# First MLP product of a diffusion step: units of 512 features, context tile as the stationary operand

## The chip, the cores and the metric

One core of a Trainium2 chip runs the whole step in one launch. The metric is the device time in microseconds (us) of one execution; lower is better. The engines are TensorE (PE in the profile; PEld is its loading of the stationary operand), VectorE (DVE), ScalarE (ACT), GpSimd (POOL) and SyncE (SP), from whose queue the DMA transfers of this kernel are issued. A matmul multiplies a stationary operand (here 128 columns, loaded into the array first) with a moving operand that streams past it column by column, and accumulates in a bank of PSUM (128 partitions x 512 float32).

## The reference

There is one layer. Its first part (norm, DeltaNet and gMLP heads, output projection) is not touched by the change. What follows it, for 128 context tokens `x` and 2048 latent tokens `y` of width 1024:

```python
h = rmsnorm(x, norm_ffn_l) * (1.0 + sc2) + sh2
x = x + ga2 * (jnp.square(jax.nn.relu(h @ w_ff1_l)) @ w_ff2_l)
...
y_prompt = rmsnorm(x, norm_final)
y_sample = rmsnorm(y, norm_final)
```

`w_ff1` is 1024 x 4096 and `w_ff2` 4096 x 1024. All is float32. The kernel reaches the accuracy with a split: each operand becomes a rounded part H and a remainder L, and a product is the three matmuls H·H, H·L and L·H (`mm3`, L214 to L220: lines 218, 219 and 220 are one matmul each, and all products of the kernel show up at these lines).

## The kernel before, in words

The tokens are 17 tiles of 128 rows: tile 0 is the context, tiles 1 to 16 are the latents. The stage in question is the first MLP product, from about 1298 us to 2023 us of the profiled span; the second MLP product follows, up to the end.

**Strassen-Winograd.** The 16 latent tiles are multiplied with seven products in place of eight. Tiles are paired (odd and even), features are split in two blocks (i = 0, 1) and the inner dimension of 1024 in two halves (kh = 0, 1). The moving operands, sums of token tiles for each of the seven products, come from DRAM as `hop` tiles (1 MB each, with parts H and L; `hop_next`, L899). Four pairs go side by side: 512 moving columns. There are two halves g of the work: g = 0 handles tiles 9 to 16, g = 1 tiles 1 to 8.

**Units.** `Unit` (L1470) takes 256 features: two blocks of 128, 16 units in each half. `loads` fetches four raw tiles of w_ff1 (one for each block and inner half; 128 x 512, 256 KB, rows of 128 floats). `weights(o)` forms the stationary operand of product o from them on DVE and splits it (`split4`, L1453: a cast on ACT, L1457, and a subtraction on DVE through the helper `add`, L1451). `product(o)` issues 4 inner tiles x 3 matmuls with the weights stationary and 512 moving columns. `step(o)` issues the product and evacuates it: copies and additions, the squared ReLU, stores to `z_d`, `s1_d` and `s2_d`, which the second MLP product reads as operands.

**The context tile.** It has no partner and is multiplied plainly, in the second half only, where the weights of a plain block are there anyway: `single` (L1566), for o in 1, 2, 0, 4, issues 12 matmuls with the weights stationary and the 128 context columns moving. Product 0 exists only for that. `single_out` applies the squared ReLU (ACT L1581, then a DVE multiplication) and stores to `z_d[0]`. `first_tile` loads the normed context tile from DRAM (`h2_0_d`) and splits it, ten steps ahead of the second half.

**Order.** `seq` (L1790) is the list of steps: for each unit its products in `ORDER` (1, 5, 6, 7, 3, 2, 4; in the second half 0 ahead of 4), the first and last units of each half two by two. At step p the loop (L1820) issues the loads of the unit that starts 14 steps later, the weights of step p + 6 (`LEAD`), the pieces of the second norm that are due, then step p and the context tile's matmuls. The second norm (`h2_steps`, L800) of tiles 8 to 0 runs inside the first half: rows (load), squares (ACT), norm2 (DVE and POOL), scale2 (DVE, L830), two groups of four transposes on PE (L837) whose evacuation `ev` (ACT, L840) adds the modulation, and for odd tiles the sums that become `hop_d`. The last sixteen steps also prepare the second product. Hop tiles of the second half are loaded around the change of halves, one every two steps, into the buffers of the first half's.

All tiles of 128 x 512 (raw weights, splits, results, the norm's rows) share the 49 buffers of the pool `wp`. SP is one queue in order, and so are ACT and DVE.

Of the kernel before, what the change touches and what calls it, by code (L numbers as in the profile page):

```python
# [52 lines left out]
LEAD = 6  # L53
ORDER = (1, 5, 6, 7, 3, 2, 4)
# [7 lines left out]
def hybrid_step(  # L62
# [43 lines left out]
    h2_d = {t: dp.tile([P, KT, P], F32, name=f"h2_{t}_d") for t in range(0, NT, 2)}  # L106
# [693 lines left out]
    def h2_steps(t, psum, tmp, wide=w512, part=None, half=None, src=None):  # L800
# [31 lines left out]
        def trans2(half):  # L832
            def f():
                ps = psum()
                ev = wide("ev")
                for i in range(4):
                    T.transpose(ps[:, i * P : (i + 1) * P], u["x"][half][:, i * P : (i + 1) * P], ident)  # L837
# [627 lines left out]
    NP = DFF // 256  # L1465
    x0 = []

    class Unit:


        def __init__(self, n):
            self.g, self.jp = divmod(n, NP)
            self.w, self.ps, self.t = {}, {}, {}

        def loads(self):
            self.raw = {}
            for kh in range(2):
                for i in range(2):
                    self.raw[i, kh] = r = as4(w512("raw"))
                    c = self.jp * 256 + i * P  # L1480
                    load(out=r, in_=w_ff1[0, kh * 512 : kh * 512 + 512, c : c + P].rearrange("(a p) c -> p a c", p=P))

        def weights(self, o):

            a, w, t = self.raw, self.w, self.t
            if o == 1:
                w[1] = split4(a[0, 0])
            elif o == 5:
                t["s"] = as4(w512("s"))
                add(t["s"], a[1, 0], a[1, 1])  # L1490
                w[5] = split4(t["s"])
            elif o == 6:
                add(t["s"], t["s"], a[0, 0], ALU.subtract)
                w[6] = split4(t["s"])
            elif o == 7:
                d = as4(w512("d"))
                add(d, a[0, 0], a[1, 0], ALU.subtract)
                w[7] = split4(d)
            elif o == 3:
                add(t["s"], a[0, 1], t["s"], ALU.subtract)  # L1500
                w[3] = split4(t["s"])
            elif o == 2:
                w[2] = split4(a[0, 1])
            elif o == 0:
                w[0] = split4(a[1, 0])
            else:
                w[4] = split4(a[1, 1])

        def product(self, o, onto=None):
            if onto is None:  # L1510
                self.ps[o] = bank()
            (h, lo), m = self.w[o], hop[self.g, o]
            mm3(self.ps[onto or o], [(h[:, kp, :], lo[:, kp, :], m[:, kp, 0, :], m[:, kp, 1, :]) for kp in range(4)],
                first=onto is None, more=onto is not None)

        def out(self, i, th, z):
            store(out=z_d[(3, 1)[self.g] + th][:, :, i, self.jp, :].rearrange("a p d -> p a d"), in_=as4(z))

        def keep(self, dst, z):
            store(out=dst[self.g][:, :, self.jp, :].rearrange("a p d -> p a d"), in_=as4(z))  # L1520

        def step(self, o):
            ps, t = self.ps, self.t
            if o == 1:
                self.product(1)
                t["x"] = w512("x")
                A.copy(t["x"], ps[1])
            elif o == 5:
                self.product(5)
                t["p5"] = w512("p5")  # L1530
                A.copy(t["p5"], ps[5])
            elif o == 6:
                self.product(6)
                add(t["x"], ps[6], t["x"])
            elif o == 7:
                self.product(7)
                t["z22"] = z = w512("p7")
                A.copy(z, ps[7])
                add(z, z, t["x"])
                add(z, z, t["p5"])  # L1540
                rl2(z, z)
                self.out(1, 1, z)
            elif o == 3:
                self.product(3, 5)
                c = w512("c12")
                add(c, ps[5], t["x"])
                rl2(c, c)
                self.out(0, 1, c)
                t["s1"] = w512("s1")
                add(t["s1"], c, t["z22"])  # L1550
                self.keep(s1_d, t["s1"])
            elif o == 2:
                self.product(2, 1)
                c = w512("c11")
                A.activation(c, ps[1], AF.Relu)
                A.activation(c, c, AF.Square)
                self.out(0, 0, c)
                s2 = w512("s2")
                add(s2, t["s1"], c, ALU.subtract)
                self.keep(s2_d, s2)  # L1560
            elif o == 4:
                self.product(4, 7)
                c = w512("c21")
                add(c, ps[7], t["x"])
                rl2(c, c)
                self.out(1, 0, c)  # L1566

        def single(self, o, ps, i, first, last):
# [9 lines left out]
    def single_out(units, ps):  # L1578
        n = 256 * len(units)
        z = w512("z0")  # L1580
        A.activation(z[:, :n], ps[:, :n], AF.Relu)  # L1581
        add(z[:, :n], z[:, :n], z[:, :n], ALU.mult)
        for i, u in enumerate(units):
            store(out=z_d[0][0, :, :, u.jp, :], in_=z[:, i * 256 : i * 256 + 256].rearrange("p (a t) -> p a t", a=2))

    def first_tile():
        x0.extend([[], []])
        for i in range(2):
            r = as4(w512("x0"))
            load(out=r, in_=h2_d[0][:, i * 4 : i * 4 + 4, :])  # L1590
            h, lo = split4(r, "x0")
            x0[0].append(h)
            x0[1].append(lo)
# [23 lines left out]
    def rows2(k, h, n):  # L1617
        return w_ff2[0, (2 * k + h) * P : (2 * k + h) * P + P, n * 512 : n * 512 + 512]
# [167 lines left out]
    blocks = [[0, 1]] + [[n] for n in range(2, NP - 2)] + [[NP - 2, NP - 1], [NP, NP + 1]]  # L1786
    blocks += [[n] for n in range(NP + 2, 2 * NP - 2)] + [[2 * NP - 2, 2 * NP - 1]]
    units = {n: Unit(n) for n in range(2 * NP)}
    seq = []
    for b in blocks:  # L1790
        order = ORDER if b[0] < NP else ORDER[:-1] + (0, 4)
        seq += [(o, n, b) for o in order for n in b]
    begun = set()

    def weights_at(p):
        if p < len(seq):
            o, n, _ = seq[p]
            units[n].weights(o)

    def loads_at(p):  # L1800
        if p < len(seq) and seq[p][1] not in begun:
            begun.add(seq[p][1])
            units[seq[p][1]].loads()
# [13 lines left out]
    later.sort(key=lambda e: e[0])  # L1817
    last = len(seq) - 16
    ps0 = None
    for p, (o, n, b) in enumerate(seq):  # L1820
# [3 lines left out]
        while later and later[0][0] <= p:  # L1824
            later.pop(0)[1]()
        if p == half - 10:
            first_tile()
        if o:
            u.step(o)
        if u.g:  # L1830
            if o == 1 and n == b[0]:
                ps0 = bank()
            u.single(o, ps0, b.index(n), o == 1 and n == b[0], o == 4 and n == b[-1])
            if o == 4 and n == b[-1]:
                single_out([units[m] for m in b], ps0)
# [3 lines left out]
        if e >= 0 and e % 2:  # L1839
# [99 lines left out]
```

## Time and profile before

| | |
|---|---|
| median of 3 runs | 2700.7 us (2700.6 to 2701.51) |
| the profiled execution | 2697.49 us, its span 2695.8 us |
| mean granted TensorE clock | 0.993 of full speed |
| bytes moved by DMA | 580.91 MB, mean 215 GB/s |

A row of a group view is: line, engine, operation, written tile <- read tiles (buffer numbers left out), shapes and count, then busy us, mean ns of one, idle time of the engine just before them and what ended it. A row of the timeline is: start and length in us, engine, line, operation; a bracket at its end gives the idle time ahead of it and the releaser. A row of the waits is: engine, line and tile <- releaser: total us, times, longest. Matmuls overlap: the length of one is its latency, and the distance from one start to the next is what it costs PE. Names: `f` is a PSUM bank of the MLP, `wH` and `wL` are the split weights, `x0H` and `x0L` the split context tile, `hop` the moving operand, `raw` a raw weight tile, `zH` and `zL` operands of the second product. The view puts operands in alphabetical order, not by their role.

### The profile page before, as it was taken

To read this page: it belongs to the slowest core of one execution; us is meant where nothing else is said; L and a number is where in the kernel's file an instruction comes from. 1 tells how busy PE (TensorE), PEld (TensorE's weight loads), DVE (VectorE), ACT (ScalarE), POOL (GpSimd) and SP (SyncE) were. 2 spreads that over 40 slices of the span, in tenths; PEclk is the share of its full clock that TensorE was granted. 3 is DMA by queue.
4 is the path that set the end of the run, shared out by engine and by line. 5 is a ranking of instruction groups with operands and counts; after the bars stand their busy time and mean duration, and the time that the engine had idled before them with its cause. 6 is when DMAs were issued, how large, how long until landed. Compare 5 with 4: busy or idle time off the path is not lost.

```text
span 2695.8 us, 45146 instructions
## 1 busy us (share of the span) xinstructions
PE 2610.2 (97%) x15682; PEld 2188.2 (81%) x15682; DVE 1868.5 (69%) x3911; ACT 1247.7 (46%) x3092; POOL 226.8 (8%) x448
## 2 busy tenths in 40 slices
PE   8999999899999889999999999999999999999998
PEld 4999998687877677778888778888888888788887
DVE  5867655867777879885678757655665546775874
ACT  4655555555555567763355533323342432332441
POOL 3112113111111111110000000000000000000000
PEclk9999999999999999999999999999999999999999
DMA  8867539555555557885877796334449978876782
GB/s 296 283 199 224 185 119 286 177 161 153 161 163 165 191 172 251 279 278 181 286 223 225 218 308 221 111 104 123 123 153 351 343 271 289 294 237 221 231 264 99
DMA packets 569387, 580.91 MB, mean 215 GB/s; under 512 B 35692, under 2 KB 401692, under 8 KB 565574
## 3 DMA queue, kind: packets, MB, share of 16 engines
q1 hardware_dynamic: 569158, 578.03, 67.0%
q8 instruction: 123, 2.02, 0.3%
q14 instruction: 106, 0.87, 0.1%
HBM read 398.14 MB, written 179.74 MB: 214 GB/s over the span
## 4 chain that ended last, share of the span: by engine, by line
PE 79%; DMA 8%; DVE 8%; ACT 2%; issue 2%; SPq 1%; POOL 0%; DVEq 0%; POOLq 0%; ACTq 0%
PE f L218 16%; PE f L220 15%; PE f L219 15%; PE pj L218 6%; PE pj L220 6%; PE pj L219 6%; PE pd L953 2%; DMA qT<-qT_d 1%; PE pm L218 1%; PE pm L220 1%; PE pm L219 1%; PE pt L569 1%; PE pd L1132 1%; PE pd L1133 1%; DMA QK<-qk_d 1%
## 5 line engine op out<-in xcount | busy, mean ns | idle before, releaser
L218 PE MATMUL f<-hop,zH 128*128 128x512 f32 x960 | 373.7, 390 | 2.2 <-ACT zH L1457 2.2
L220 PE MATMUL f<-hop,zL 128*128 128x512 f32 x960 | 373.9, 390 | 1.9 <-DVE zL L1451 1.7
L219 PE MATMUL f<-hop,zH 128*128 128x512 f32 x960 | 373.2, 389 | 0.0
L218 PE MATMUL f<-hop,wH 128*128 128x512 f32 x896 | 355.4, 397 | 6.1 <-ACT wH L1457 6.1
L220 PE MATMUL f<-hop,wL 128*128 128x512 f32 x896 | 350.7, 392 | 0.0
L219 PE MATMUL f<-hop,wH 128*128 128x512 f32 x896 | 350.3, 391 | 0.0
L1457 ACT CAST zH<-zraw 128x512 fp32r<-128x512 f32 x240 | 147.5, 621 | 294.0 <-DMA zraw<-s_d 93.3
L220 PEld LDWEIGHTS f<-hop,zL 128*128 128x128 f32 x960 | 180.2, 188 | 43.2 <-DVE zL L1451 4.3
L218 PEld LDWEIGHTS f<-hop,zH 128*128 128x128 f32 x960 | 180.2, 188 | 42.1 <-ACT zH L1457 3.1
L1451 DVE TENSOR_TENSOR zL<-zraw,zH 128x512 fp32r<-128x512 f32 x240 | 163.3, 688 | 70.3 <-ACT zH L1457 55.4
L219 PEld LDWEIGHTS f<-hop,zH 128*128 128x128 f32 x960 | 180.2, 188 | 37.2
L218 PEld LDWEIGHTS f<-hop,wH 128*128 128x128 f32 x896 | 169.5, 189 | 39.6 <-ACT wH L1457 6.5
L220 PEld LDWEIGHTS f<-hop,wL 128*128 128x128 f32 x896 | 169.0, 189 | 37.4 <-DVE wL L1451 0.3
L219 PEld LDWEIGHTS f<-hop,wH 128*128 128x128 f32 x896 | 169.5, 189 | 33.9
L220 PE MATMUL pj<-kH,wL 128*128 128x386 f32 (+2 forms) x568 | 190.5, 335 | 0.0
L218 PE MATMUL pj<-kH,wH 128*128 128x386 f32 (+2 forms) x568 | 189.3, 336 | 0.3 <-DVE kH L467 0.3
L219 PE MATMUL pj<-kL,wH 128*128 128x386 f32 (+2 forms) x568 | 189.2, 333 | 0.0
L177 POOL TENSOR_TENSOR r<-rsq,nhalf 128x1 f32<-128x1 f32 (+1 forms) x38 | 22.8, 599 | 1504.7 <-DVE rsq L176 1504.7
L1451 DVE TENSOR_TENSOR wL<-raw,wH 128x512 fp32r<-128x512 f32 x112 | 76.2, 688 | 75.5 <-ACT wH L1457 71.1
L517 DVE SCALAR_TENSOR_TENSOR cv<-pj,vec,cv 128x384 f32<-128x384 f32 (+2 forms) x164 | 87.3, 540 | 57.5 <-ACT cv L514 56.1
L218 PEld LDWEIGHTS pj<-kH,wH 128*128 128x128 f32 x568 | 107.0, 189 | 4.7 <-issue 4.2
L219 PEld LDWEIGHTS pj<-kL,wH 128*128 128x128 f32 x568 | 107.4, 189 | 0.5
(404 smaller groups left out, 6074.8 us busy)
## 6 DMA issues: line engine op xcount, KB each, us to landing
zraw<-z_d SPq DMA_DIRECT2D x212, 256.0 KB
raw<-in_w_ff_dram SPq DMA_DIRECT2D x128, 256.0 KB
hop<-hop_d SPq DMA_DIRECT2D x28, 1024.0 KB
z_d<-c SPq DMA_DIRECT2D x96, 256.0 KB
zraw<-s_d SPq DMA_DIRECT2D x96, 256.0 KB
raw<-in_w_mod_dram SPq DMA_DIRECT2D x80, 256.0 KB
r<-in_w_ff_dram SPq DMA_DIRECT2D x80, 256.0 KB
s_d<-s SPq DMA_DIRECT2D x64, 256.0 KB
```

Source lines behind the costliest of these rows:

```text
L177: G.tensor_tensor(out=out, in0=t[:np_, :n], in1=nhalf[:np_, :n], op=ALU.pow)
L218: T.matmul(ps, lh, rh, start=first and i == 0, stop=False, skip_group_check=more)
L219: T.matmul(ps, lh, rl, start=False, stop=False, skip_group_check=more)
L220: T.matmul(ps, ll, rh, start=False, stop=last and i == n - 1, skip_group_check=more)
L517: V.scalar_tensor_tensor(out=cv[:, o : o + m], in0=ps[:, s + sh : s + sh + m], scalar=convw[:, w, j : j + 1], in1=cv[:, o : o + m], op0=AL ...
L569: T.matmul(ps[:, i * P : (i + 1) * P], kTt[:, i * P : (i + 1) * P], rhs[:, i * P : (i + 1) * P], start=True, stop=True)
L953: T.matmul(p[:, h, :], lhs[:, h, :], rhs[:, h, :], start=True, stop=True)
L1132: T.matmul(p[:, h, :], u["qT"][:, h, :], s[:, h, :], start=True, stop=False)
L1133: T.matmul(p[:, h, :], u["QK"][:, h, :], u["vn"][:, h, :], start=s is None, stop=True)
L1451: V.tensor_tensor(out=out, in0=a, in1=b, op=op)
L1457: A.copy(h, src)
```

## The change

- A unit now takes 512 features: two blocks of 256 (i), each two groups of 128 (m); 8 units in each half. A step is (product o, unit n, group m), so there are as many steps as before. A raw tile holds 256 inner rows x 256 columns (still 256 KB, in rows of 256 floats), eight for a unit; the two inner quarters are called q. `weights(o, q)` is built at the place of step (o, m = q), and a product needs both quarters. `LEAD` is 5. The loads of a unit are spread over its first four steps, 13 steps ahead.
- `single` has the context tile stationary and the weights of block i moving, 256 columns, two inner tiles x 3 matmuls for each quarter, into one bank for a whole unit (tokens on partitions, 512 features along). ACT applies the ReLU. Four steps into the next unit, `turn` transposes the four 128 x 128 blocks on PE, and ACT squares them out of PSUM for the store.
- The context tile no longer goes through DRAM: its norm hands `ev` to `own_tile`, which splits it at once; `first_tile` is gone.
- Product 2 moves ahead of 6 (and so does its hop load), and c11 is kept until product 3 forms s1 and s2. In the second half 0 stands between 6 and 7.
- The second norm: rows, squares, norm2 and scale2 come two steps earlier each; the transposes and what follows stay where they were.
- `rows2` maps the rows of w_ff2 to the new order of features. The units are no longer taken two by two.

```diff
-LEAD = 6
-ORDER = (1, 5, 6, 7, 3, 2, 4)
+LEAD = 5
+ORDER = (1, 5, 2, 6, 7, 3, 4)
+ORDER1 = (1, 5, 2, 6, 0, 7, 3, 4)
...
-                if t in h2_d:
+                if own:
+                    own(ev, half)
+                elif t in h2_d:
                     store(out=h2_d[t][:, half * 4 : half * 4 + 4, :], in_=ev.rearrange("p (k d) -> p k d", k=4))
...
-    NP = DFF // 256
-    x0 = []
+    NP = DFF // 512
+    x0 = {}
...
+        def load(self, i, kh):
+            for q in range(2):
+                self.raw[i, kh, q] = r = w512("raw")
+                r0, c0 = kh * 512 + q * 256, self.jp * 512 + i * 256
+                load(out=r.rearrange("p (a c) -> p a c", a=2),
+                     in_=w_ff1[0, r0 : r0 + 256, c0 : c0 + 256].rearrange("(a p) c -> p a c", p=P))
+
+        def loads(self, o, m):
+            if o in (1, 5):
+                self.load(*{(1, 0): (0, 0), (1, 1): (1, 0), (5, 0): (1, 1), (5, 1): (0, 1)}[o, m])
+
+        def weights(self, o, q):
+
+            a = {(i, kh): self.raw[i, kh, q] for i in range(2) for kh in range(2)}
...
+        def product(self, o, m, onto=None):
             if onto is None:
-                self.ps[o] = bank()
+                self.ps[o, m] = bank()
+            cs, mv, trip = slice(m * P, m * P + P), hop[self.g, o], []
+            for kp in range(4):
+                h, lo = self.w[o, kp // 2]
+                trip.append((h[:, kp % 2, cs], lo[:, kp % 2, cs], mv[:, kp, 0, :], mv[:, kp, 1, :]))
+            mm3(self.ps[onto or o, m], trip, first=onto is None, more=onto is not None)
...
-            c = (2 * i + (o in (0, 4))) * P
-            k0 = 4 * (o in (2, 4))
-            h, lo = self.w[o]
-            mm3(ps[:, c : c + P], [(h[:, kp, :], lo[:, kp, :], x0[0][k0 // 4][:, kp, :], x0[1][k0 // 4][:, kp, :])
-                                   for kp in range(4)], first=first, last=last)
...
+            if o == 1 and q == 0:
+                self.ps0 = bank()
+            i, kh = int(o in (0, 4)), int(o in (2, 4))
+            h, lo = self.w[o, q]
+            xh, xl = x0[kh]
+            mm3(self.ps0[:, i * 256 : i * 256 + 256],
+                [(xh[:, 2 * q + j, :], xl[:, 2 * q + j, :], h[:, j, :], lo[:, j, :]) for j in range(2)],
+                first=o == 1 and q == 0, last=o == 4 and q == 1)
+            if o == 4 and q == 1:
+                self.z0 = w512("z0")
+                A.activation(self.z0, self.ps0, AF.Relu)
+
+        def turn(self):
+
+            ps = bank()
+            for i in range(4):
+                T.transpose(ps[:, i * P : (i + 1) * P], self.z0[:, i * P : (i + 1) * P], ident)
+            z = w512("zt")
+            A.activation(z, ps, AF.Square)
+            store(out=z_d[0][0, :, :, 2 * self.jp : 2 * self.jp + 2, :],
+                  in_=z.rearrange("p (i m t) -> p i m t", i=2, m=2))
...
+    seq = [(o, n, m) for n in range(2 * NP) for o in (ORDER if n < NP else ORDER1) for m in range(2)]
...
+    def own_tile(ev, i):
+        x0[i] = split4(as4(ev), "x0")
+
     later = []
     for j, t in enumerate(range(8, -1, -1)):
-        st = h2_steps(t, bank, lambda: w512("junk"), w512)
+        st = h2_steps(t, bank, lambda: w512("junk"), w512, own=own_tile if t == 0 else None)
         p = 10 + 19 * j // 2
-        later += [(p - (3 if k == 0 else 0) + k, st[k]) for k in range(len(st))]
+        later += [(p + (-5, -1, 0, 1)[k] if k < 4 else p + k, j, k, st[k]) for k in range(len(st))]
...
-        if p == half - 10:
-            first_tile()
...
         if u.g:
...
+            u.single(o, m)
+            if o == 4 and m:
+                turns[p + 4] = u
+            if p in turns:
+                turns.pop(p).turn()
...
+    for u in turns.values():
+        u.turn()
```

More of the change, by code (lines that the diff above doesn't have):

```diff
@@ L798, in hybrid_step, with h2_steps @@
     bs = vec[:, 69:73]
-    def h2_steps(t, psum, tmp, wide=w512, part=None, half=None, src=None):
+    def h2_steps(t, psum, tmp, wide=w512, part=None, half=None, src=None, own=None):
         u = {}
@@ L1472, in __init__ @@
             self.g, self.jp = divmod(n, NP)
[L1473 to L1485, printed above, removed]
+            self.w, self.ps, self.t, self.raw = {}, {}, {}, {}
@@ L1510, in product @@
+        def product(self, o, m, onto=None):
             if onto is None:
-                self.ps[o] = bank()
[L1512 to L1520, printed above, removed]
@@ L1522, in step, with out @@
-        def step(self, o):
+                self.ps[o, m] = bank()
[4 more added lines that the diff above has]
+            mm3(self.ps[onto or o, m], trip, first=onto is None, more=onto is not None)
+        def out(self, i, th, m, z):
+            store(out=z_d[(3, 1)[self.g] + th][:, :, i, 2 * self.jp + m, :].rearrange("a p d -> p a d"), in_=as4(z))
@@ L1523, in step, with keep @@
+        def keep(self, dst, m, z):
+            store(out=dst[self.g][:, :, 2 * self.jp + m, :].rearrange("a p d -> p a d"), in_=as4(z))
+        def step(self, o, m):
             ps, t = self.ps, self.t
             if o == 1:
-                self.product(1)
-                t["x"] = w512("x")
-                A.copy(t["x"], ps[1])
+                self.product(1, m)
+                t["x", m] = w512("x")
+                A.copy(t["x", m], ps[1, m])
             elif o == 5:
-                self.product(5)
@@ L1530, in step @@
-                t["p5"] = w512("p5")
-                A.copy(t["p5"], ps[5])
+                self.product(5, m)
+                t["p5", m] = w512("p5")
+                A.copy(t["p5", m], ps[5, m])
+            elif o == 2:
+                self.product(2, m, 1)
+                t["c11", m] = c = w512("c11")
+                A.activation(c, ps[1, m], AF.Relu)
+                A.activation(c, c, AF.Square)
+                self.out(0, 0, m, c)
             elif o == 6:
-                self.product(6)
@@ L1534, in step @@
-                add(t["x"], ps[6], t["x"])
+                self.product(6, m)
+                add(t["x", m], ps[6, m], t["x", m])
             elif o == 7:
[L1536 to L1540, printed above, removed]
+                self.product(7, m)
+                t["z22", m] = z = w512("p7")
+                A.copy(z, ps[7, m])
+                add(z, z, t["x", m])
+                add(z, z, t["p5", m])
@@ L1541, in step @@
                 rl2(z, z)
-                self.out(1, 1, z)
+                self.out(1, 1, m, z)
             elif o == 3:
-                self.product(3, 5)
+                self.product(3, m, 5)
                 c = w512("c12")
-                add(c, ps[5], t["x"])
+                add(c, ps[5, m], t["x", m])
                 rl2(c, c)
[L1548 to L1557, printed above, removed]
+                self.out(0, 1, m, c)
@@ L1558, in step @@
+                s1 = w512("s1")
+                add(s1, c, t["z22", m])
+                self.keep(s1_d, m, s1)
                 s2 = w512("s2")
-                add(s2, t["s1"], c, ALU.subtract)
-                self.keep(s2_d, s2)
+                add(s2, s1, t["c11", m], ALU.subtract)
+                self.keep(s2_d, m, s2)
             elif o == 4:
-                self.product(4, 7)
+                self.product(4, m, 7)
                 c = w512("c21")
-                add(c, ps[7], t["x"])
+                add(c, ps[7, m], t["x", m])
@@ L1565, in step, with single @@
                 rl2(c, c)
-                self.out(1, 0, c)
-        def single(self, o, ps, i, first, last):
+                self.out(1, 0, m, c)
+        def single(self, o, q):
             if o not in (1, 2, 0, 4):
                 return
-            c = (2 * i + (o in (0, 4))) * P
-            k0 = 4 * (o in (2, 4))
-            h, lo = self.w[o]
-            mm3(ps[:, c : c + P], [(h[:, kp, :], lo[:, kp, :], x0[0][k0 // 4][:, kp, :], x0[1][k0 // 4][:, kp, :])
-                                   for kp in range(4)], first=first, last=last)
@@ L1578, in single_out @@
[L1578 to L1593, printed above, removed]
+            if o == 1 and q == 0:
+                self.ps0 = bank()
@@ L1596, in hybrid_step, with split2 @@
+    def split2(src):
+        h = wp.tile([P, 2, 256], F32R, tag="w", name="wH")
+        lo = wp.tile([P, 2, 256], F32R, tag="w", name="wL")
+        s2 = src.rearrange("p (a c) -> p a c", a=2)
+        A.copy(h, s2)
+        add(lo, s2, f32(h), ALU.subtract)
+        return h, lo
     pairs = [(9 + 2 * i, 10 + 2 * i) for i in range(4)] + [(1 + 2 * i, 2 + 2 * i) for i in range(4)]
@@ L1783, in s_next @@
                 sops[m] = s_build(*raws.pop(m))
-    blocks = [[0, 1]] + [[n] for n in range(2, NP - 2)] + [[NP - 2, NP - 1], [NP, NP + 1]]
-    blocks += [[n] for n in range(NP + 2, 2 * NP - 2)] + [[2 * NP - 2, 2 * NP - 1]]
     units = {n: Unit(n) for n in range(2 * NP)}
[L1789 to L1793, printed above, removed]
+    seq = [(o, n, m) for n in range(2 * NP) for o in (ORDER if n < NP else ORDER1) for m in range(2)]
     def weights_at(p):
         if p < len(seq):
-            o, n, _ = seq[p]
-            units[n].weights(o)
+            o, n, m = seq[p]
+            units[n].weights(o, m)
     def loads_at(p):
-        if p < len(seq) and seq[p][1] not in begun:
-            begun.add(seq[p][1])
-            units[seq[p][1]].loads()
+        if p < len(seq):
+            o, n, m = seq[p]
+            units[n].loads(o, m)
     for p in range(LEAD + 8):
@@ L1824, in hybrid_step @@
         while later and later[0][0] <= p:
-            later.pop(0)[1]()
-        if p == half - 10:
-            first_tile()
+            later.pop(0)[3]()
         if o:
-            u.step(o)
+            u.step(o, m)
         if u.g:
[L1831 to L1835, printed above, removed]
+            u.single(o, m)
[3 more added lines that the diff above has]
+                turns.pop(p).turn()
         if half - 11 <= p < half + 3 and (half - p) % 2:
```

39 lines of the change are left out of this document (20 added, 19 removed).

## The prediction

> **What bounds the kernel now.** I read the page from the top: busy shares, then the chain of waits, then the groups of instructions.
>
> ```profile
> span 2695.8 us, 45146 instructions
> PE 2610.2 (97%) x15682; PEld 2188.2 (81%) x15682; DVE 1868.5 (69%) x3911; ACT 1247.7 (46%) x3092; POOL 226.8 (8%) x448
> PE 79%; DMA 8%; DVE 8%; ACT 2%; issue 2%; SPq 1%; POOL 0%; DVEq 0%; POOLq 0%; ACTq 0%
> ```
>
> PE is busy for 97% of the span and carries 79% of the chain. So time falls where PE gets fewer or cheaper matmuls, or where PE waited. Next I cut the first MLP product out with the windows view: its first half (tiles 9 to 16) and its second half (tiles 1 to 8, and the context tile). The columns are length, busy time of PE, weight loads, DVE, ACT and POOL, granted clock, DMA share and GB/s.
>
> ```profile
> 1298.60:1632.40 333.80, 321.11 (x1430) 264.35 (x1429) 243.02 (x407) 156.62 (x325) 5.65 (x9) 0.98 0.83 261
> 1632.40:2022.98 390.58, 390.58 (x2102) 335.80 (x2101) 244.13 (x385) 130.33 (x239) 0.00 (x0) 1.00 0.46 135
> ```
>
> The second half has no idle PE at all: only its matmuls count. The first half has 333.80 - 321.11 = 12.69 us idle. Both run 16 x 7 products of 12 matmuls over 512 columns. The second half adds the context tile, 16 x 4 x 12 = 768 matmuls over 128 columns:
>
> ```profile
> L220 PE MATMUL f<-x0H,wL 128*128 128x128 f32 x256 | 70.7, 276 | 0.0
> L219 PE MATMUL f<-x0L,wH 128*128 128x128 f32 x256 | 70.3, 275 | 0.0
> L218 PE MATMUL f<-x0H,wH 128*128 128x128 f32 x256 | 67.7, 264 | 0.0
> ```
>
> The 276 ns are latency, since matmuls overlap. The price is the distance from start to start, which the timeline gives:
>
> ```profile
> 1800.24 0.39 PE L220 MATMUL f<-hop,wL 128*128 128x512 f32 x1
> ...
> 1800.47 0.22 PE L218 MATMUL f<-x0H,wH 128*128 128x128 f32 x1
> ...
> 1801.65 0.28 PE L220 MATMUL f<-x0H,wL 128*128 128x128 f32 x1
> ...
> 1801.76 0.45 PE L218 MATMUL f<-hop,wH 128*128 128x512 f32 x1
> ...
> 1802.05 0.40 PE L219 MATMUL f<-hop,wH 128*128 128x512 f32 x1
> ```
>
> Twelve narrow matmuls take 1801.76 - 1800.47 = 1.29 us, 0.108 each, and the first wide one behind them takes 0.29 us instead of the usual distance. That usual distance is 0.227 us:
>
> ```profile
> 1983.75 0.39 PE L219 MATMUL f<-hop,wH 128*128 128x512 f32 x1
> ...
> 1989.65 0.39 PE L218 MATMUL f<-hop,wH 128*128 128x512 f32 x1
> ```
>
> There are 26 distances between these two rows, 5.90 us, 0.2269 each. So 1344 wide matmuls are 305.0 us, one product (a "step" below) is 2.72 us, and of the second half 390.58 - 305.0 = 85.6 us belong to the context tile (1.34 per block of twelve).
>
> **The change: the context tile's matmuls.** Removed: 85.6 us. Added: 8 units x 8 steps x 6 = 384 matmuls over 256 columns. This shape is not in the trace; the nearest row is the input projection at 258 columns:
>
> ```profile
> 388.22 0.28 PE L218 MATMUL pj<-kH,wH 128*128 128x258 f32 x1
> ...
> 390.05 0.28 PE L218 MATMUL pj<-kH,wH 128*128 128x258 f32 x1
> ```
>
> 15 distances in 1.83 us, 0.122 each. 384 x 0.122 = 46.8 us. The lower end is the narrow matmul's 0.108 (41.5 us), the upper end twice that, the same time per column as now (82.9 us). I take 0.122, because that row has the same element type, the same number of weight columns and almost the same width. Between the kinds of matmul there may be a seam: the 0.29 above is 0.06 too long, x64 = 4.0 us at most, nothing at least. I take 1.3, since a 256-column stream covers most of the next weight load (the 258-column one runs slower than the narrow one, so it is not waiting for weights).
>
> **Transposes.** Eight units get four each, behind the fourth step of the next unit. The nearest rows are those of the second norm:
>
> ```profile
> 1562.57 0.39 PE L220 MATMUL f<-hop,wL 128*128 128x512 f32 x1
> 1562.82 1.09 PE L837 MATMUL f<-ident,x 128*128 128x128 f32 x8
> 1563.67 0.47 PE L218 MATMUL f<-hop,wH 128*128 128x512 f32 x1
> 1563.98 0.39 PE L219 MATMUL f<-hop,wH 128*128 128x512 f32 x1
> ```
>
> Eight transposes hold PE for 0.85 us, 0.106 each, plus 0.08 at the seam behind them; four cost 0.5, so 8 x 0.5 = 4.0 us. At worst each costs the whole latency of a narrow matmul, 0.276: 8.8; at best they lie in a wait and cost nothing. I take 4.0, the row of the same operation. The Trainium skill ("TensorE: Matmul & The Clock Gate", Part 4: PE-mode transpose) reports about 275 ns for one transpose inside a kernel. The trace does not agree that this is the price: eight in a row span 1.09 us and not 2.2. By it the 32 would be an estimated 8.8 us, and the sum 4.8 us worse.
>
> The transposes wait for ACT's Relu, which is four steps (10.9 us) old by then. Only the last unit's come directly behind its own Relu, at the end of the stage. There ACT is done at 2023.78 and PE would have gone on at 2022.98:
>
> ```profile
> 2022.98 0.45 PE L218 MATMUL f<-hop,zH 128*128 128x512 f32 x1
> ...
> 2023.18 0.60 ACT L1581 ACTIVATE z<-f 128x512 f32<-128x512 f32 x1 [9.08 <-PE f L220]
> ```
>
> That is 0.8, with the hand-over 1.1 us; nothing if other products are placed ahead. I take 1.1. Second half: 85.6 - 46.8 - 1.3 - 4.0 - 1.1 = 32.4 us gained.
>
> **The context tile stays on chip.** Now its second norm goes to DRAM and comes back; the two reloads sit in SP's queue between the hop loads, and ACT, which works in order, stands before their split:
>
> ```profile
> 1607.24 0.62 ACT L1457 CAST x0H<-x 128x512 fp32r<-128x512 f32 x1 [12.22 <-issue]
> 1617.82 0.62 ACT L1457 CAST x0H<-x 128x512 fp32r<-128x512 f32 x1 [9.96 <-DMA x<-h_d]
> ```
>
> Behind it the weights' casts are late, and PE stands:
>
> ```profile
> 1619.01 0.80 PE L218 MATMUL f<-hop,wH 128*128 128x512 f32 x1 [6.09 <-ACT wH L1457]
> 1619.60 0.63 PE L219 MATMUL f<-hop,wH 128*128 128x512 f32 x1
> ...
> 1624.30 0.44 PE L218 MATMUL f<-hop,wH 128*128 128x512 f32 x1
> ```
>
> ```profile
> 1620.00:1625.00 5.00, 5.00 (x14) 3.98 (x14) 5.00 (x9) 2.01 (x4) 0.00 (x0) 0.56 0.22 90
> ```
>
> 6.09 us idle, and then the granted clock is down: from 1619.01 to 1624.30 twelve matmuls take 5.29 us instead of 12 x 0.227 = 2.72, another 2.57. With the split straight behind the norm on ACT, there is nothing from DRAM to wait for: 8.7 us go. The four casts and subtractions remain, some twelve steps earlier, where ACT has room (156.62 of 333.80 us). Two 256 KB stores and two loads leave SP's queue.
>
> **The second norm gets an earlier start.** Its load, squares, norm and scaling come two steps earlier, its transposes do not. The rest of the idle time is transposes waiting for that scaling:
>
> ```profile
> PE f L837 <- DVE x L830: 6.6, 3, 4.5
> ```
>
> ```profile
> 1504.81 1.05 PE L837 MATMUL f<-ident,x 128*128 128x128 f32 x4 [4.48 <-DVE x L830]
> ...
> 1508.52 0.40 PE L219 MATMUL f<-hop,wH 128*128 128x512 f32 x1
> ```
>
> ```profile
> 1335.00:1340.00 5.00, 4.06 (x20) 3.11 (x20) 3.59 (x8) 4.97 (x13) 0.55 (x1) 1.00 1.07 312
> ```
>
> The longest is 4.48 us, with a slow clock behind it: four transposes (0.45) and seven matmuls (1.59) take 3.71, which is 1.67 too much. The other two (6.6 - 4.5 = 2.1) cost only themselves; around one of them the clock is 1.00. The Trainium skill (same page, "What's actually happening") says that the clock halves after an idle window of about 3.4 us. The trace agrees: 4.48 and 6.09 us brought it down, 0.94 us did not. In all, the rows leave 4.48 + 1.67 + 2.1 = 8.3 us to win. Two steps, 5.44 us, exceed the longest wait; yet DVE is busy for 243.02 of 333.80 us and may push the norm back. I take 7.0, between 0 and 8.3.
>
> **What costs nothing, and its cover.** A product now needs two half builds, and LEAD falls from 6 to 5, so the later half is built four steps ahead instead of six. The shortest margin in the first half, away from the standstill, is this build (the 96th) and its first use:
>
> ```profile
> 1565.01 0.68 DVE L1451 TENSOR_TENSOR wL<-s,wH 128x512 fp32r<-128x512 f32 x1
> ...
> 1575.13 0.39 PE L220 MATMUL f<-hop,wL 128*128 128x512 f32 x1
> ```
>
> 1575.13 - 1565.69 = 9.4 us; less two steps, 4.0 remain. If that were gone, a product would wait for its DVE subtraction. Builds, evacuations and loads keep number and size (128 loads of 256 KB, in rows of 1 KB instead of 512 B); the squaring moves from DVE to ACT, neither of which PE waits for in the second half. Order 2 ahead of 6 only swaps two hop loads of equal size and equal distance. More wide tiles are alive at once. By my count of the 49 buffers, raw weights hold 9.7 on average (two tiles of each of four blocks for 17, 16, 19 and 16 steps, over a unit's 14), splits 13, results 5, the norm 10 and the context tile 4: 42.
>
> **Sum.** 32.4 + 8.7 + 7.0 = 48.1 us. The profiled execution took 2697.49 (span 2695.8); after it 2649.4. The median of the runs lies 3.2 above that execution: 2652.6.
>
> **Rivals.** *A standstill at the change of halves remains.* SP is one queue, and hop loads wait in it until PE releases a buffer:
>
> ```profile
> SPq L903 <- PE f L220: 23.3, 5, 13.4
> ```
>
> In the second half's first unit, the last raw tiles now go behind the first hop load in that queue; their build comes eight steps, 21.8 us, later. A hold of 13.4 and a slow landing (the reload above made ACT wait 9.96) make 23.4, and the build 1.6 us late; ACT and all casts behind it wait too. It decides once that is more than the margin of 4.0. A standstill like the 4.48 us one, with its clock, costs 6.2; if the norm's waits stay too, another 7.0. Time: 2658.8 to 2665.8. Against it: in the 13.4 us hold PE was itself standing still.
>
> *A 256-column matmul costs as much per column as a 128-column one*, 0.216: 82.9 us instead of 46.8, time 2688.7. The 258-column rows speak against it.
>
> *Slower than before: the wide buffers run out.* If raw tiles and kept results exceed 49, a raw load waits for a buffer, the split is late and PE stands once per unit. A wait like the 4.48 us one costs 6.15 with its clock; 16 units: 98 us, time 2751. It decides when a raw load comes later than the eight steps (21.8 us) up to its build and the margin of 4.0 behind it; it is slower than before from 8 units on. Against it: 7 buffers are spare by my count. For it: DVE, busy 73% of the first half, delays releases.
>
> **How the numbers follow.** Forecast 0.70, standstill 0.21, per-column price 0.03, buffers 0.06 (0.01 of it with so few units that the time is unchanged). So faster 0.94, same 0.01, slower 0.05; same means within 0.2%, 5.4 us, about what a measurement of this kernel can tell. The lower end has all of the norm's 8.3 us gone (1.3 more), no seam and no wait at the end (2.4) and 0.108 per matmul (46.8 - 41.5 = 5.3): 48.1 + 9.0 = 57.1 gained, 2643.6; I take 2642, for the timeline's rows are rounded. The upper end is the standstill at 2665.8 with the full seam (2.7) and most of the doubt on transposes (3.5 of 4.8): 2672.
>
> **What would show it.** Right: the second half without idle PE and about 358 us long; 256-column rows 0.12 us apart; no wait above 1 us at L837; no row for a reload of the context tile, no clock below 0.9 in the stage. Wrong: idle PE behind late casts of raw tiles; 256-column rows at 0.2; a new long wait between the halves.

## The result, and the profile after

| | before | after |
|---|---|---|
| median | 2700.97 us (2700.6 to 2701.51, 4 runs) | 2654.38 us (2652.01 to 2654.97, 4 runs) |
| profiled execution, span | 2697.49, 2695.8 us | 2653.89, 2652.1 us |
| ratio | | 0.9826, 95% interval 0.9809 to 0.9843 |

The changed kernel is faster by 1.7%; the forecast was 2652.6 us, from 2642 to 2672. First the head of the page after, where the share of PE is the same 97% of a shorter span:

```profile
span 2652.1 us, 44445 instructions
PE 2575.7 (97%) x15330; PEld 2155.1 (81%) x15330; DVE 1858.1 (70%) x3897; ACT 1247.4 (47%) x3094; POOL 229.1 (9%) x448
```

Then the windows view, cut at the same places as before: the first wide matmul of the stage, the first matmul of the context tile, the first matmul of the second MLP product.

```profile
1296.97:1621.55 324.58, 319.15 (x1429) 263.52 (x1428) 246.27 (x414) 156.08 (x330) 9.43 (x9) 0.99 0.81 260
1621.55:1975.31 353.76, 353.07 (x1749) 299.03 (x1748) 233.54 (x367) 130.28 (x237) 0.00 (x0) 1.00 0.50 151
1975.31:2652.10 676.79, 662.93 (x2891) 541.45 (x2889) 427.78 (x695) 229.35 (x420) 11.14 (x17) 0.99 0.78 260
```

The same cuts before, with fewer columns (length, busy time of PE, clock, DMA share, GB/s):

```profile
1298.77:1632.53 333.76, 321.07 (x1429) 0.98 0.83 261
1632.53:2022.98 390.45, 390.45 (x2101) 1.00 0.46 135
2022.98:2695.80 672.82, 659.99 (x2890) 1.00 0.77 260
```

So the change of 43.7 us in the span divides into: ahead of the stage -1.8; first half 333.8 to 324.6, -9.2; second half 390.5 to 353.7, -36.7 (rounded); second MLP product 672.8 to 676.8, +4.0. So the second half gained more than forecast (32.4), the first half less (15.7), and a part that the change does not touch took 4.0 back. The prices in the second half can be read from the timeline after, one block of the context tile between two wide matmuls:

```profile
1747.33 0.39 PE L221 MATMUL f<-hop,wL 128*128 128x512 f32 x1
1747.55 0.28 PE L219 MATMUL f<-wH,x0H 128*128 128x256 f32 x1
1747.67 0.28 PE L220 MATMUL f<-wL,x0H 128*128 128x256 f32 x1
...
1748.15 0.28 PE L221 MATMUL f<-wH,x0L 128*128 128x256 f32 x1
1748.27 0.40 PE L219 MATMUL f<-hop,wH 128*128 128x512 f32 x1
1748.50 0.40 PE L220 MATMUL f<-hop,wH 128*128 128x512 f32 x1
```

Six matmuls of 256 columns take 1748.27 - 1747.55 = 0.72 us, 0.120 each, and the wide matmuls on both sides keep their usual distance (0.22 and 0.23): there is no seam. 384 x 0.120 = 46.1 us.

The waits view of PE for the whole stage after has two rows:

```profile
PE f L219 <- ACT p L1553: 5.4, 1, 5.4
PE f L1597 <- ACT z L1591: 0.7, 1, 0.7
```

The second is the last unit's transposes behind their own Relu, forecast with 1.1. The first was not forecast. The four old waits of the first half (6.6 us at the transposes, 6.1 at the weights) are gone, and a new one stands in the stage's first unit. On PE's, SP's and ACT's timelines it looks like this:

```profile
1332.10 0.39 PE L221 MATMUL f<-hop,wL 128*128 128x512 f32 x1
1337.90 0.79 PE L219 MATMUL f<-hop,wH 128*128 128x512 f32 x1 [5.41 <-ACT p L1553]
1338.49 0.63 PE L220 MATMUL f<-hop,wH 128*128 128x512 f32 x1
```

```profile
1299.02 9.12 SPq L906 DMA_DIRECT2D hop<-hop_d  x10
1310.31 19.75 SPq L1482 DMA_DIRECT2D raw<-in_w_ff_dram  x8
1330.43 1.09 SPq L811 DMA_DIRECT2D x<-x_d  x2
```

```profile
1330.44 0.62 ACT L1607 CAST wH<-raw 128x512 fp32r<-128x512 f32 x1 [6.84 <-DMA raw<-in_w_ff_dram]
1336.04 0.63 ACT L818 ACTIVATE junk<-x 128x512 f32<-128x512 f32 x1 [4.98 <-DMA z_d<-p]
...
1337.28 0.56 ACT L1553 COPY p<-f 128x512 f32<-128x512 f32 x1
```

PE wants to accumulate product 4 onto product 7's bank and waits for ACT to copy that bank (L1553). ACT has stood for 4.98 us ahead of the squares of tile 8's second norm (`junk<-x`), and those wait for rows that SP issued only at 1330.43, since the eight raw tiles ahead of them took 19.75 us behind ten hop loads. (The row names a store to z_d as the releaser; the load of `x` is what the squares read, and the run with the rows first, below, bears that out.) Behind the wait the matmuls are 0.43 us apart for a while, so it costs about 8 us. The granted clock from 1338 to 1343 us is 0.50.

### The profile page after: what moved, and what is told of

It is laid out like the page before. It is cut to its first block, busy times and chain, and to the rows that moved or that the text cites. A ratio compares the mean times of both kernels' runs of the same rounds, so it can differ in the third digit from the quotient of the medians.

```text
span 2652.1 us, 44445 instructions
## 1 busy us (share of the span) xinstructions
PE 2575.7 (97%) x15330; PEld 2155.1 (81%) x15330; DVE 1858.1 (70%) x3897; ACT 1247.4 (47%) x3094; POOL 229.1 (9%) x448
## 4 chain that ended last, share of the span: by engine, by line
PE 78%; DMA 11%; DVE 7%; issue 2%; SPq 1%; ACT 1%; POOL 0%; DVEq 0%; POOLq 0%; ACTq 0%
PE f L219 14%; PE f L221 14%; PE f L220 14%; PE pj L219 6%; PE pj L221 6%; PE pj L220 6%; PE pd L956 2%; DMA qT<-qT_d 2%; DMA r<-in_w_ff_dram 2%; PE pm L219 1%; PE pm L221 1%; PE pm L220 1%; PE pm L316 1%; PE pt L570 1%; PE pd L1135 1%
## 5 line engine op out<-in xcount | busy, mean ns | idle before, releaser
L221 PE MATMUL f<-hop,wL 128*128 128x512 f32 x896 | 345.2, 391 | 0.0
L220 PEld LDWEIGHTS f<-hop,wH 128*128 128x128 f32 x896 | 169.1, 189 | 32.4
L1607 ACT CAST wH<-s 128x512 fp32r<-128x512 f32 x96 | 59.0, 622 | 156.6 <-DVE s L1454 152.0
```

What stands on the lines that cost most here:

```text
L220: T.matmul(ps, lh, rl, start=False, stop=False, skip_group_check=more)
L221: T.matmul(ps, ll, rh, start=False, stop=last and i == n - 1, skip_group_check=more)
L1607: A.copy(h, s2)
```

## The experiments

Stage lengths below are those of each run's profile, cut as above. The runs are from three groups, each measured beside the kernel before on one chip, where that one had a median of 2697.7, 2700.26 and 2697.81 us; single executions of one kernel lie up to 12 us apart, so stage lengths tell more than totals.

**Tile 8's norm at its old place** (first guess at the new wait: the norm's new place in ACT's order).

```diff
-        later += [(p + (-5, -1, 0, 1)[k] if k < 4 else p + k, j, k, st[k]) for k in range(len(st))]
+        sh = (-3, 1, 2, 3) if j == 0 else (-5, -1, 0, 1)
+        later += [(p + sh[k] if k < 4 else p + k, j, k, st[k]) for k in range(len(st))]
```

> The changed kernel, with the second norm of tile 8 alone (the first one, j = 0) at its places of before: load, squares, norm2 and scale2 two steps later. Theory: the new standstill of 5.41 us at 1332 us is ACT, in order, waiting with tile 8's squares for rows that were loaded behind eight raw tiles, while the copy that frees the bank of product 7 stands behind it. Then the standstill and its slow clock (2.6 us) go: 2646 us, no wait of PE above 1.5 us in the first half. Rival: the raw tiles of the second unit, late behind the ten hop loads, would stop ACT in any case; then a wait of 4 to 6 us stays within 20 us of that place and the time stays at 2652 to 2655.

Measured: 2655.97 us (2651.17 to 2657.3), ratio 0.9843 (0.9828 to 0.9857). The first half is 324.7 us as in the changed kernel. The wait changed its name, not its length:

```profile
PE f L838 <- DVE x L831: 5.8, 1, 5.8
```

Now the transposes of tile 8 wait for the scaling of the same late rows. The order on ACT is not the cause, so this theory fell; what both have in common is the late load, which the last runs below put to the test.

**All norms at their old places** (the same line with (-3, 1, 2, 3) for every tile).

> The changed kernel, with the second norms of all tiles at their places of before. Theory: the standstill at 1332 us goes (8 us), and the waits of transposes for the scaling come back, 8.3 us of them with the slow clock: 2652 to 2656 us. Rival: those waits came from the old order of products and not from the norm's place; then L837's transposes wait for less than 2 us and the time is near 2646.

Measured: 2674.25 us (2671.06 to 2677.34), ratio 0.9914 (0.9899 to 0.9928). First half 343.1 us, 18.5 more than the changed kernel. The waits came back, and more of them than the kernel before had:

```profile
PE f L838 <- DVE x L831: 12.1, 4, 5.8
PE f L219 <- ACT x L1536: 6.5, 1, 6.5
```

So the early start of the norms is worth 18.5 us in the new order; the 6.6 us of waits in the kernel before (8.3 with their slow clock) understate it. Both expected times were too low. Why the waits grow in the new order was not tried.

**Weights stationary again**, within the new units.

```diff
-            mm3(self.ps0[:, i * 256 : i * 256 + 256],
-                [(xh[:, 2 * q + j, :], xl[:, 2 * q + j, :], h[:, j, :], lo[:, j, :]) for j in range(2)],
-                first=o == 1 and q == 0, last=o == 4 and q == 1)
+            for m in range(2):
+                c, cs = (2 * i + m) * P, slice(m * P, m * P + P)
+                mm3(self.ps0[:, c : c + P],
+                    [(h[:, j, cs], lo[:, j, cs], xh[:, 2 * q + j, :], xl[:, 2 * q + j, :]) for j in range(2)],
+                    first=o == 1 and q == 0 and m == 0, last=o == 4 and q == 1 and m == 1)
...
-            ps = bank()
-            for i in range(4):
-                T.transpose(ps[:, i * P : (i + 1) * P], self.z0[:, i * P : (i + 1) * P], ident)
             z = w512("zt")
-            A.activation(z, ps, AF.Square)
+            A.activation(z, self.z0, AF.Square)
```

> The changed kernel, with the roles of the operands for the context tile as before: the weights stationary, the context tile moving with 128 columns (768 matmuls), no transposes at the end. Theory: the second half's gain is nearly all the wider moving operand: 85.6 us in place of 46.8 + 4.0, so the second half is 33 to 36 us longer than the changed kernel's 353.8, and the time 2686 to 2692. Rival: the larger units, the spread loads and the other order gave a good part of it; then the time is below 2680.

Measured: 2689.51 us (2684.04 to 2693.93, 7 runs), ratio 0.9968 (0.9957 to 0.998). The second half is back near the 390.5 us of the kernel before:

```profile
1620.55:2011.47 390.92, 390.92 (x2101) 1.00 0.45 139
```

So the larger units, the spread loads and the new order give nothing there: 37.2 us hang on the matmuls of the context tile alone.

**Roles exchanged, but 128 columns.** The same loop over m, with the context tile stationary and `h[:, j, cs]`, `lo[:, j, cs]` moving; the transposes stay.

> The changed kernel, with the context tile stationary as in the change, but the weights moving 128 columns at a time instead of 256 (768 matmuls again; the transposes stay). It parts the exchange of roles from the width. Theory: only the width pays, since a 128-column matmul cost 0.108 to 0.111 us in the kernel before, whichever operand stood still, and a 256-column one 0.120 in the changed kernel: the second half grows from 353.7 by 768 x 0.11 - 384 x 0.12 = 38 us to about 392, the time to 2692. Rival: a stationary context tile is itself cheaper (the same weight columns are loaded again and again); then the second half stays below 380 us.

Measured: 2695.65 us (2693.3 to 2700.44, 10 runs), ratio 0.9993 (0.9984 to 1.0002): no gain left over the kernel before. The second half:

```profile
1623.63:2019.21 395.58, 394.89 (x2133) 1.00 0.45 137
```

That is 41.8 us more than with 256 columns (38 expected). The exchange of roles pays only because it lets one matmul move 256 columns. By itself it costs: the second half is 4.7 us longer than with the weights stationary, 3.4 of it for the transposes (next run).

**Every transpose twice.** `for _ in range(2)` around the transpose.

> The changed kernel, with every transpose of the context tile's result done twice (64 instead of 32, the second over the first). Theory: a transpose costs PE 0.11 us, so the second half is 3.5 us longer than 353.7 and the time 2657 to 2659. Rival (each costs its latency, 0.27 us): 8.8 us longer.

Measured: 2657.46 us (2655.85 to 2658.59), ratio 0.9839 (0.9823 to 0.9856); second half 357.15 us against 353.74, so 32 more transposes cost 3.4 us, 0.107 each. Their latency is not their price.

**The context tile through DRAM again**: `h2_0_d`, and `first_tile` ten steps ahead of the second half, as in the kernel before.

> The changed kernel, with the context tile stored to DRAM after its norm and loaded and split ten steps ahead of the second half, as before. Theory: the reload stands between the hop loads in SP's queue, ACT waits for it, and the standstill of 4 to 9 us with its slow clock is back: 2659 to 2664 us. Rival: with the loads of a unit spread over its steps the reload comes through in time (or LEAD's build margin covers it): 2652 to 2655.

Measured: 2669.84 us (2668.59 to 2673.77), ratio 0.99 (0.9885 to 0.9915). First half 342.6 us, 18.0 more than in the changed kernel. The first row here is the waits view, the others are ACT's timeline:

```profile
PE f L219 <- ACT wH L1607: 17.6, 1, 17.6
```

```profile
1606.54 0.62 ACT L1460 CAST x0H<-x 128x512 fp32r<-128x512 f32 x1 [14.56 <-DMA x<-h_d]
1622.04 0.62 ACT L1460 CAST x0H<-x 128x512 fp32r<-128x512 f32 x1 [14.89 <-DMA x<-h_d]
```

The mechanism is the one forecast (ACT, in order, before a reload from behind the hop loads). It costs more than expected and more than the 8.7 us of the kernel before: ACT stands 14.56 and 14.89 us ahead of the two splits here, 12.22 and 9.96 there. Why it is longer in the new order was not tried.

**The first half's two edits alone, in the kernel before**: the split straight from the norm and the earlier norms; units of 256, weights stationary.

> The kernel before, with two edits alone: the context tile is split straight from its norm (no reload), and the second norms start two steps earlier. Units of 256, weights stationary. Theory: these two are the first half's whole gain; the waits of 6.1 and 6.6 us with their slow clock go, unless the early rows of tile 8 are late here too: 17 us less without such a wait, 9 with one, so a ratio to the kernel before of 0.9937 to 0.9967. Rival: the units of 512 and the spread loads carry the first half's gain; then the ratio is above 0.998.

Measured: 2682.67 us (2678.02 to 2685.99), ratio 0.9934 (0.9917 to 0.995). The first half has no wait at all:

```profile
1304.06:1620.08 316.02, 316.02 (x1430) 1.00 0.85 266
```

That is 17.8 us less than before; 17.0 had been counted as the most there was (8.7 + 8.3). In this kernel SP issues tile 8's rows ahead of the next raw tiles:

```profile
1306.09 9.15 SPq L905 DMA_DIRECT2D hop<-hop_d  x10
1317.41 2.81 SPq L810 DMA_DIRECT2D x<-x_d  x2
1323.49 11.39 SPq L1483 DMA_DIRECT2D raw<-in_w_ff_dram  x4
```

So the two edits do what was forecast. The changed kernel's first half is 8.6 us longer than this one; that most of it is the rows behind eight raw tiles of the larger units is shown by the next runs.

**Tile 8's rows first.** All norms are made ahead of the loop, and the row load of tile 8 is issued before the stage's first loads.

```diff
+    norms = {t: h2_steps(t, bank, lambda: w512("junk"), w512, own=own_tile if t == 0 else None) for t in range(9)}
+    norms[8][0]()
     for p in range(LEAD + 8):
         loads_at(p)
...
+    later = [e for e in later if e[1:3] != (0, 0)]
```

> The changed kernel, with the two row loads of tile 8's second norm issued before the first loads of the stage, ahead of the ten hop loads and the second unit's raw tiles in SP's queue. New theory, after the run that moved tile 8's norm: its place in the order is not the cause; the rows are issued only at about 1330 us, because the eight raw tiles ahead of them are held 19 us behind the hop loads, and whatever needs the rows next waits. Then no wait of PE above 1 us is left in the first half, the first half is 316 to 317 us long instead of 324.6, and the time is 8 us below the changed kernel's of the same call or of its own runs (2646). Rival: the second unit's raw tiles, as late as the rows, stop ACT and then PE by themselves; then a wait of over 3 us is left near 1335 us and nothing is gained.

Measured: 2646.86 us (2643.7 to 2655.85), ratio 0.9808 (0.9785 to 0.983); first half 317.3 us, the longest wait of PE in it 0.2 us. The raw tiles are as late as ever, and no longer wait of PE comes of it. Since its executions lay 12 us apart, it was measured once more beside the changed kernel on one chip.

> The changed kernel once more, beside the next one on the same chip: 2652 to 2656 us, with the standstill of 4 to 6 us in the stage's first unit.

> The changed kernel with tile 8's rows loaded ahead of the stage's first loads, once more, beside the changed kernel on the same chip. Theory: 6 to 9 us less than that one, by the standstill of the first unit and its slow clock alone (first half 317 us in place of 324). Rival: the earlier run's gain came from another chip's spread; then the two agree within 3 us.

Measured: 2652.42 us (2652.29 to 2653.97), ratio 0.9832 (0.9819 to 0.9846), for the changed kernel, and 2645.06 us (2638.05 to 2649.09), ratio 0.98 (0.9783 to 0.9818), with the rows first: 7.4 us less. The windows (length, PE busy, clock, DMA share, GB/s) of the first half, the changed kernel and then the rows first:

```profile
1296.61:1619.80 323.19, 319.13 (x1429) 0.99 0.81 261
```

```profile
1302.56:1620.02 317.46, 316.99 (x1429) 1.00 0.82 264
```

5.7 us are in the first half; another 4.0 are in the second MLP product (677.0 and 673.0 us), where this edit changes nothing (see the last section). Against that, the stage begins 6.0 us later in this profile (1302.56 against 1296.61), so the two spans differ by 3.6 only. Nearly all of this lag comes ahead of the edit: 5.7 of it are there already at the last store that SP issues before the moved row load (L1325, 1255.07 against 1249.38). Both profiles with the rows first are of the slowest execution of their run. The intervals of the two ratios just part, at 0.9818 and 0.9819; with the stage lengths (317.3 and 317.5 against 324.6 and 323.2 in the two profiles of the changed kernel) a gain of 5.7 to 7.3 us in the first half is shown, and this is the best version found.

**LEAD 4**: weights built four steps ahead instead of five, all loads where they were.

> The changed kernel, with the weights of a step built four steps ahead instead of five; raw loads and hop loads stay where they are. The prediction had 4.0 us of margin left for the later quarter; the changed kernel's trace has only 0 to 1 us at the worst places of the first half. Theory: the cover is used up, so one step (2.72 us) less brings waits of PE for weights at some ten to twenty places of the first half, 10 to 40 us: 2664 to 2695 us. Rival (the prediction's margin holds): no such waits, 2652 to 2656 us.

Measured: 2653.53 us (2653.07 to 2658.82), ratio 0.9831 (0.9816 to 0.9846); first half 322.5 us, no new wait of PE in it. In the second half (354.8 us, 1.0 more) one short wait for a weights' cast appears, at 1958 us:

```profile
PE f L219 <- ACT wH L1607: 0.5, 1, 0.5
```

The theory fell: ten to twenty such waits were expected. Its margins of 0 to 1 us came from pairing builds and products by their count, and some came out negative, which no real margin can be, so such pairs mean nothing.

## Why the prediction was right, point by point

**The context tile's matmuls: right, a little too careful.** 384 x 0.122 = 46.8 us was forecast from the 258-column rows; 0.120 and 46.1 us were measured. The seam, taken at 1.3, is nothing. With the narrow moving operand in place of the wide one all of the gain is gone, so the reason, the width, is shown, and not only the sum. What in a 128-column matmul costs 0.108 us, when the next 128 columns add 0.012, is not shown; the prediction's words on the weight load are an argument.

**Transposes: right.** 4.0 us forecast, 3.4 measured by doubling. The other price, 0.27 us each, would have made the doubled run 8.8 us longer. At the end of the stage PE waits 0.7 for the Relu, not 1.1. Together with the seam's 1.3 and another 1.3 us that rows rounded to 0.01 us cannot place, the second half gained 36.7 instead of 32.4.

**Context tile kept on chip, and earlier norms: the mechanisms were right, the balance of the first half was not.** Both old waits went, as the run with these edits alone shows (17.8 us). The step of the sum that failed is "8.7 + 7.0" for the first half: it measured 9.2. The step in the text behind it is the sentence that loads "keep number and size" and so cost nothing. Number and size stayed, but their place in SP's queue changed: eight raw tiles now stand between the hop loads and tile 8's rows, and the new wait, with its slow clock, cost about 8 us for which the sum had no term. That the rows are also asked for two steps earlier made no difference (tile 8's norm at its old place). One of the signs named ahead failed with it: the clock did go below 0.9 in the stage. The forecast had looked for such a queue only at the change of halves, where nothing happened; it was at the start of the stage. Its first rival had the mechanism (a load held in SP's queue behind hop loads) and the size (6.2 us for a 4.48 us wait) at the wrong place.

**LEAD and the later builds: right in the result, not in the reason.** No product waited for its build; with LEAD 4 one did, for 0.5 us. But the 9.4 us margin in the forecast rests on the same counting of pairs that failed above, so the number is not to be trusted.

**Rivals.** Price per column: excluded by the 0.120. Buffers running out: no wait for a raw tile's buffer reached PE. The standstill at the change of halves: not there, PE has no wait between 1340 and 1970 us.

**The sum** was 4.4 us off in the span, with errors of both signs: the second half gained 4.3 more and the first half 6.5 less than forecast, the stretch ahead of the stage gave 1.8 and the second MLP product took 4.0, neither of them forecast. That these errors nearly cancel is luck: the second half as measured and the first as forecast would have given 6.5 us less. The median is only 1.8 off the forecast, since it lies 0.5 above this profile's time and not 3.2.

## What to carry to other kernels

Look at what a matmul costs by its number of moving columns: here 0.108 us for 128, 0.120 for 256 and 0.227 for 512, each with a weight load of its own. When a thin operand (128 rows here) meets wide weights, let the thin one stand still and move the wide one, and turn the result afterwards; here 12 matmuls of 128 columns, 1.34 us, became 6 of 256, 0.72 us, and the transposes gave back a tenth of the gain. When loads are regrouped, read the order in each DMA queue and not only their bytes: what is asked for next to a burst should be issued ahead of it. A wait that moves to another name when its supposed cause is removed (5.4 us at a copy, 5.8 us at a transpose) may have its cause further up; here it was a load.

## What the runs showed of the hardware that was not expected

Behind two short waits close together the granted clock can be down, and not in every execution. In the second MLP product PE waits twice at the same place in all profiles, with two matmuls in between. Before:

```profile
2309.77 0.50 PE L218 MATMUL f<-hop,zH 128*128 128x512 f32 x1 [1.05 <-ACT zH L1457]
2310.11 0.40 PE L219 MATMUL f<-hop,zH 128*128 128x512 f32 x1
2312.25 0.50 PE L220 MATMUL f<-hop,zL 128*128 128x512 f32 x1 [1.75 <-DVE zL L1451]
2312.59 0.39 PE L218 MATMUL f<-hop,zH 128*128 128x512 f32 x1
```

After:

```profile
2263.57 0.50 PE L219 MATMUL f<-hop,zH 128*128 128x512 f32 x1 [1.10 <-ACT zH L1460]
2263.90 0.40 PE L220 MATMUL f<-hop,zH 128*128 128x512 f32 x1
2266.05 0.80 PE L221 MATMUL f<-hop,zL 128*128 128x512 f32 x1 [1.75 <-DVE zL L1454]
2266.64 0.63 PE L219 MATMUL f<-hop,zH 128*128 128x512 f32 x1
```

After the same two waits the matmuls follow at 0.43 us here and at 0.23 there. The windows view of PE (length, busy time, clock, DMA share, GB/s), after and then before:

```profile
2265.31:2270.31 5.00, 4.26 (x10) 0.50 0.99 343
```

```profile
2312.98:2317.98 5.00, 5.00 (x21) 1.00 1.01 344
```

Of the thirteen profiles, nine have a granted clock of 0.50 to 0.72 in the 5 us behind the two waits and four (the kernel before, LEAD 4, the first half's two edits, the doubled transposes) 1.00. The prediction's reading, by which it takes one long wait to bring the clock down (4.48 and 6.09 us did, 0.94 did not), is too simple: it was down behind 1.10 and 1.75 us. What decides in a single execution was not tried.

This place is most of the 4.0 us that the second MLP product "lost". Between the two profiles PE is busy 2.9 us longer for about the same number of matmuls (the slower clock) and idle 1.0 us longer. Some 10 us ahead of the two waits there is a third one, of 1.32 us at 2253.77, which the profile before does not have; it stands, with 0.95 to 1.33 us, in seven of the thirteen. The part is 672.8 to 677.0 us long over all profiles, 677.0 and 676.8 in the two of the changed kernel, which have the third wait and the low clock both. Others have one without the other (LEAD 4 the third wait alone, tile 8's norm at its old place the low clock alone), in work that the edits do not touch, so a good part of the 4.0 us comes and goes between executions; whether the changed kernel makes it more likely is left open.
